# Moving the split weight tiles by 16 bytes, and the attention outputs by 128, within the scratch memory of a decoder trunk

## The chip, the cores and the metric

The kernel runs on one core of one Trainium2 chip. The metric is the device time in microseconds of one execution; the time before is the median of three runs, 2121.67 us (2117.71 to 2123.2).

## The reference

Two layers of a decoder trunk over 512 tokens of width 1024, one sequence. Each layer is a half-step SwiGLU FFN (hidden width 2816), a token mixer with three head groups in parallel (gated linear attention, native sparse attention, RetNet), and a second half-step FFN. Each sub-layer reads an RMS-normed, modulated input and adds a gated result; the modulation (nine vectors a layer) comes from a conditioning vector.

```
for l in range(2):
    mod = silu(c) @ w_ada[l] + b_ada[l]            # 9 x 1024
    x += 0.5 * gt1 * swiglu(modulate(rms_norm(x)), ffn1_in, ffn1_out)
    x += gtm * token_mixer(modulate(rms_norm(x)), w_in, ..., w_out)
    x += 0.5 * gt2 * swiglu(modulate(rms_norm(x)), ffn2_in, ffn2_out)
return rms_norm(x, final_norm_g)
```

All of it is float32.

## The kernel before, in words

Activations are kept transposed: `x` is 128 partitions by 8 chunks of the width by 512 tokens. The large products are done in TensorE's rounded float32 type (F32R) with a split: each operand is a rounded high part and a low part (the rest), and a product is three matmuls, high by high, high weight by low input, low weight by high input (`mm3`, lines 414 to 420). The inputs are split once into `hh`, `hl` (normed input), `gh`, `gl` (FFN hidden), `oh`, `ol` (linear attention outputs) and `nh`, `nl` (sparse attention outputs).

Weights come in units of 128 by 1024, some smaller. The class `Weights` streams them in the order of a list: `dma_to` loads a unit from DRAM into one of three `wraw` buffers on the SP queue; `split_to` rounds it on ScalarE into one of four `whi` buffers (line 170) and subtracts on VectorE, for a few units on GpSimd, into one of four `wlo` buffers (line 171). A unit is split two units ahead of its use, so there are normally 24 matmuls, eight slices of 128 weight columns by three, for each pair of split instructions. In an FFN, each unit's slices are the stationary operand and a 128x512 chunk of the input is the moving one. In the projections of `proj_n` (lines 578 to 580) and the small ones at 643 to 645 the roles are swapped: slices of the input are stationary, and `whi` and `wlo` move. Around the norms, FFN and output products run in halves of 256 tokens.

The order within an engine is that of the program, with a planner's priorities; tiles are laid out by pools in the 128 partitions' scratch memory, one after the other, in byte offsets common to all partitions. Constants come first from the left, then the `weights` pool (three wraw, four whi, four wlo, 4096 bytes a partition each), then `hh` and `hl`, then the pools of a stage. The FFN's pool (`gh`, `gl`), the mixer's `mix` pool and the `lin` pool (`oh`, `ol`, `nh`, `nl`) are laid out from the right end. In this layout the offsets modulo 256 are:

| tiles | offset modulo 256 |
|---|---|
| wraw, whi, wlo | 128 |
| hh, hl, gh, gl | 128 |
| qraw, qrot, krot, vnat, oh, ol, nh, nl | 0 |

The slices of a tile are 512 bytes (weights) or 1024 and 2048 bytes (inputs) apart, so all slices of a tile share its class; the exception is the units of lines 643 to 645, whose slices are 1696 bytes apart. `G` (the sparse attention's gates) uses 96 of the 120 elements it is given; it is the first tile of the `mix` pool from the right.

`load_consts` loads the constants; its later part (`late`) is built behind the first products: DMAs on GpSimd's queue, a cast of the causal mask to bf16, memsets. `onat` holds the natural-order outputs of the two linear attentions; `lin_evac` writes it first, at line 859.

Of the kernel before, what the change touches and what calls it, by code (L numbers as in the profile page):

```python
# [7 lines left out]
F32 = mybir.dt.float32  # L8
F32R = mybir.dt.float32r
# [9 lines left out]
L, D, T, F = 2, 1024, 512, 2816  # L19
# [120 lines left out]
class Weights:  # L140
# [21 lines left out]
    def split_to(self, i):  # L162
        while self.ns < len(self.units) and self.ns <= i:
            j = self.ns
            self.dma_to(j)
            _, w, pool = self.units[j]
            r = self.raw.pop(j)
            h = self.pool.tile([128, D], F32R, name="whi", tag="whi", bufs=self.b)
            lo = self.pool.tile([128, D], F32R, name="wlo", tag="wlo", bufs=self.b)
            self.nc.scalar.activation(h[:, :w], r[:, :w], AF.Copy)  # L170
            (self.nc.gpsimd if pool else self.nc.vector).tensor_tensor(lo[:, :w], r[:, :w], h[:, :w].bitcast(F32),  # L171
                                                                       op=ALU.subtract)
            self.hl[j] = (h[:, :w], lo[:, :w])
            self.ns += 1
# [11 lines left out]
class Build:  # L186
# [19 lines left out]
    def load_consts(self):  # L206
        nc, cp, a = self.nc, self.const, self.a
        self.ones = cp.tile([128, 128], F32, name="ones")
        nc.vector.memset(self.ones, 1.0)
        self.scratch = cp.tile([128, 1], F32, name="scratch")  # L210
        self.eps = cp.tile([128, 1], F32, name="eps")
        nc.vector.memset(self.eps, EPS)

        def ld0(key, shape, dt=F32, eng=None):
            t = cp.tile(shape, dt, name="k_" + key)
            (eng or nc.scalar).dma_start(t, a[key])
            return t

        self.ident = ld0("k_ident", [128, 128])
        self.bada = ld0("bada", [128, L, NADA * KC])  # L220
        self.ng = ld0("ng", [128, L, 3, KC])

        def late():
            def ld(key, shape, dt=F32):
                return ld0(key, shape, dt, nc.gpsimd)

            self.fng = ld("fng", [128, KC])
            self.kd = ld("k_kd", [128, 4])
            self.gc = ld("k_gc", [128, 2])
            self.cma = ld("k_cma", [128, 4, 32])  # L230
            self.cmm = ld("k_cmm", [128, 32])
            self.ab = ld("ab", [128, L, 2])
            causal = ld("k_causal", [128, 128])
            self.causal = cp.tile([128, 128], BF16, name="causal")
            nc.gpsimd.tensor_copy(self.causal, causal)
            self.identb = cp.tile([128, 128], BF16, name="identb")
            nc.gpsimd.tensor_copy(self.identb, self.ident)
            self.vb = cp.tile([128, 4, 128], F32, name="vb")
            nc.gpsimd.memset(self.vb, 0.0)
            self.hv = cp.tile([128, 2, 2, 32], F32, name="hv")  # L240
            nc.gpsimd.memset(self.hv, 0.0)
            self.onat = cp.tile([128, 4, 2, 256], F32, name="onat")
            self.sg = cp.tile([128, 4, 2, 256], F32, name="sg")
            self.stats = cp.tile([128, 2, 2, 4, 2], F32, name="stats")
            self.kcT = cp.tile([128, 2, 32], F32, name="kcT")
            nc.gpsimd.memset(self.kcT, 0.0)
        self.late_consts = late
# [346 lines left out]
    def mixer(self, l):  # L594
        nc, tc = self.nc, self.tc
        self.mp_cm = tc.tile_pool(name="mix", bufs=1, side="right", reuse_waits="tile")
        mp = self.mp = self.mp_cm.__enter__()
# [1 line left out]
        qrot = mp.tile([128, 4, T], F32, name="qrot")  # L599
        krot = mp.tile([128, 2, T], F32, name="krot")  # L600
        vnat = mp.tile([128, 4, 256], F32, name="vnat")
        G = mp.tile([128, 120], F32, name="G")[:, 0:96].rearrange("p (c k) -> p c k", c=4)
        onat, sg, stats = self.onat, self.sg, self.stats
        with tc.tile_pool(name="mtmp", bufs=1, reuse_waits="tile") as tp:
            self.tp = tp
# [54 lines left out]
            for c in range(4):  # L660
                nc.vector.tensor_tensor(G[:, c, :], gl[:, c, 0:24], gb, op=ALU.add)
            nc.scalar.activation(G, G, AF.Exp, scale=-1.0)
            nc.vector.tensor_scalar(G, G, 1.0, None, op0=ALU.add)
            nc.vector.reciprocal(G, G)
            self.dbg(f"G{l}", G)
            self.dbg(f"kcT{l}", self.kcT)
# [12 lines left out]
            for pr in range(2):  # L679
                e = tp.tile([128, T], F32, name="e", tag="e", bufs=1)  # L680
                q = tp.tile([128, T], F32, name="rq", tag="rq", bufs=2)
                k = tp.tile([128, T], F32, name="rk", tag="rk", bufs=2)
                p = self.proj_t(l, f"gq{pr}")
                nc.scalar.activation(q, p, AF.Copy, scale=0.125)
                p = self.proj_t(l, f"gk{pr}")
# [8 lines left out]
            for pr in range(2):  # L694
                q = tp.tile([128, T], F32, name="rq", tag="rq", bufs=2)
                k = tp.tile([128, T], F32, name="rk", tag="rk", bufs=2)
                for t, n, s in ((q, "rq", 1.0), (k, "rk", 0.125)):
                    p = self.proj_t(l, f"{n}{pr}")
# [3 lines left out]
            for i, n in enumerate(("ks", "kw")):  # L702
                p = self.proj_t(l, n)
                raw = tp.tile([128, T], F32, name="raw", tag="raw", bufs=2)
                self.rotary(p, krot[:, i, :], raw, 1.0)
            for i in range(4):
                p = self.proj_t(l, f"nq{i}")
# [6 lines left out]
        self.ol = op.tile([128, 4, T], F32R, name="ol")  # L714
        self.nsa(l, qraw, qrot, krot, vnat, G)

# [526 lines left out]
```

## Time and profile before

| what | value |
|---|---|
| median of the runs | 2121.67 us |
| the profiled execution's own time | 2122.84 us |
| its span, first to last instruction | 2121.1 us |
| TensorE matmul busy | 2093.0 us, 99% |
| weight loads busy | 1743.2 us, 82% |
| VectorE, ScalarE, GpSimd busy | 52%, 38%, 10% |
| HBM read over the span | 124 GB/s with the writes |

A matmul's row in the profile has a duration that overlaps with the next one's, since matmuls are pipelined; two matmuls' starts give the time that one takes in a stream. The starts are in the timeline, in steps of 0.01 us, so a step is taken over several rows.

### The profile page before, as it was taken

The numbers are of one execution on the slowest core, as the hardware profiler recorded it, in microseconds if no ns is written. First come the engines' busy times: TensorE is split into PE (matmuls) and PEld (weight loads), VectorE is DVE, ScalarE is ACT, GpSimd is POOL, SyncE is SP. The second block draws the span as 40 slices with busy tenths as digits, with TensorE's granted clock in tenths as the row PEclk, the third lists the DMA queues.
The fourth block names the chain that finished last, engine by engine and source line by source line (L and its number), as shares of the span: only waits on it lengthen the run. The fifth ranks groups of instructions, "written<-read, shape, count | busy, mean of one in ns | idle before, by whom it ended". The sixth has DMA issues, their size and how long they took to land.

```text
span 2121.1 us, 27803 instructions
## 1 busy us (share of the span) xinstructions
PE 2093.0 (99%) x10938; PEld 1743.2 (82%) x10938; DVE 1108.0 (52%) x1731; ACT 796.3 (38%) x1309; POOL 211.0 (10%) x196
## 2 busy tenths in 40 slices
PE   9999999999999999999999999999999999999998
PEld 7888888988965988888888888889788669888887
DVE  8894333637875799533353333335578754333332
ACT  4422323543665522222342222234527654222323
POOL 1000001312301200000110000012223020000002
PEclk9999999999999999999999999999999999999999
DMA  9894323423310699432333233235232112233322
GB/s 342 310 358 156 91 83 100 144 90 96 96 40 19 236 359 339 159 99 78 91 110 93 82 114 99 75 98 166 82 90 79 31 35 85 91 89 113 96 80 80
DMA packets 93829, 269.10 MB, mean 127 GB/s; under 512 B 10865, under 2 KB 21985, under 8 KB 93698
## 3 DMA queue, kind: packets, MB, share of 16 engines
q1 hardware_dynamic: 92018, 266.06, 38.7%
q8 instruction: 86, 1.41, 0.3%
q0 software_dynamic: 672, 0.58, 0.2%
q10 hardware_dynamic: 1008, 0.69, 0.1%
q14 instruction: 45, 0.37, 0.0%
HBM read 259.94 MB, written 2.10 MB: 124 GB/s over the span
## 4 chain that ended last, share of the span: by engine, by line
PE 96%; DVE 2%; ACT 1%; issue 1%; POOL 0%; DMA 0%; POOLq 0%; DVEq 0%; ACTq 0%
PE mm L418 26%; PE mm L419 26%; PE mm L420 26%; PE o L1062 2%; PE mm L579 1%; PE t L1052 1%; PE mm L578 1%; PE mm L580 1%; PE mm L1020 1%; PE f L419 1%; PE f L418 1%; PE f L420 1%; PE mm L1021 1%; DVE hl L349 0%; PE o L756 0%
## 5 line engine op out<-in xcount | busy, mean ns | idle before, releaser
L170 ACT ACTIVATE whi<-wraw 128x1024 fp32r<-128x1024 f32 (+3 forms) x374 | 361.1, 966 | 1054.8 <-PE mm L419 971.8
L419 PE MATMUL mm<-hl,whi 128*128 128x512 f32 (+1 forms) x1736 | 654.8, 378 | 3.1 <-DVE hl L349 3.1
L420 PE MATMUL mm<-hh,wlo 128*128 128x512 f32 (+1 forms) x1736 | 654.5, 378 | 0.0
L418 PE MATMUL mm<-hh,whi 128*128 128x512 f32 (+1 forms) x1736 | 649.3, 378 | 2.8 <-ACT hh L378 2.2
L171 DVE TENSOR_TENSOR wlo<-wraw,whi 128x1024 fp32r<-128x1024 f32 (+2 forms) x354 | 390.7, 1104 | 447.7 <-ACT whi L170 440.6
L419 PEld LDWEIGHTS mm<-hl,whi 128*128 128x128 f32 x1736 | 328.6, 189 | 62.4 <-DVE hl L349 3.7
L418 PEld LDWEIGHTS mm<-hh,whi 128*128 128x128 f32 x1736 | 326.5, 189 | 64.0 <-issue 3.1
L420 PEld LDWEIGHTS mm<-hh,wlo 128*128 128x128 f32 x1736 | 328.3, 189 | 60.5 <-issue 2.0
L419 PE MATMUL mm<-gl,whi 128*128 128x512 f32 (+1 forms) x792 | 290.2, 366 | 0.0
L420 PE MATMUL mm<-gh,wlo 128*128 128x512 f32 (+1 forms) x792 | 289.6, 366 | 0.0
L418 PE MATMUL mm<-gh,whi 128*128 128x512 f32 (+1 forms) x792 | 289.1, 365 | 0.0
L301 POOL TENSOR_TENSOR sqa<-sqa,sq 128x512 f32<-128x512 f32 (+1 forms) x44 | 51.3, 1165 | 1433.2 <-ACT sq L300 1125.8
L544 DVE TENSOR_TENSOR sg<-sg,mm 128x512 f32<-128x512 f32 x85 | 58.4, 687 | 227.5 <-PE mm L420 225.0
L256 DVE SCALAR_TENSOR_TENSOR adaw<-adaw,cact 128x1024 f32<-128x1024 f32 x144 | 171.7, 1217 | 6.6 <-ACT cact L1150 6.6
L419 PEld LDWEIGHTS mm<-gl,whi 128*128 128x128 f32 x792 | 149.4, 189 | 24.3
L420 PEld LDWEIGHTS mm<-gh,wlo 128*128 128x128 f32 x792 | 149.4, 189 | 24.0
L418 PEld LDWEIGHTS mm<-gh,whi 128*128 128x128 f32 x792 | 149.4, 189 | 24.0
L426 DVE SCALAR_TENSOR_TENSOR x<-mm,mod,x 128x512 f32<-128x512 f32 (+1 forms) x94 | 63.0, 671 | 136.5 <-PE mm L420 136.5
L1027 ACT ACTIVATE p<-mm,nm 128x128 f32<-128x128 f32 (+3 forms) x128 | 66.4, 532 | 18.9 <-DVE nm L1024 18.7
L579 PE MATMUL mm<-wlo,hh 128*128 128x256 f32 x256 | 72.9, 285 | 0.0
L578 PE MATMUL mm<-whi,hh 128*128 128x256 f32 x256 | 72.9, 285 | 0.0
L580 PE MATMUL mm<-whi,hl 128*128 128x256 f32 x256 | 72.7, 284 | 0.0
(289 smaller groups left out, 2145.2 us busy)
## 6 DMA issues: line engine op xcount, KB each, us to landing
wraw<-wfi SPq DMA_DIRECT2D x176, 512.0 KB, 3.7
adaw<-wada SPq DMA_DIRECT2D x144, 512.0 KB, 5.6
wraw<-wfo SPq DMA_DIRECT2D x64, 384.0 KB, 3.1
wraw<-wfo SPq DMA_DIRECT2D x64, 320.0 KB, 2.9
wraw<-wt SPq DMA_DIRECT2D x30, 512.0 KB, 3.7
wraw<-wn SPq DMA_DIRECT2D x16, 512.0 KB, 3.8
w<-w SPq DMA_DIRECT2D x16, 256.0 KB, 5.3
wraw<-wol SPq DMA_DIRECT2D x8, 512.0 KB, 3.7
```

The costliest lines, as they stand in the source:

```text
L170: self.nc.scalar.activation(h[:, :w], r[:, :w], AF.Copy)
L171: (self.nc.gpsimd if pool else self.nc.vector).tensor_tensor(lo[:, :w], r[:, :w], h[:, :w].bitcast(F32), op=ALU.subtract)
L256: i = nc.vector.scalar_tensor_tensor(w, w, 1.0, self.cact, op0=ALU.mult, op1=ALU.mult, accum_out=self.mod[l][:, f:f + 1])
L418: nc.tensor.matmul(out, wh[:, wk], hh[:, hk], start=start, stop=False)
L419: nc.tensor.matmul(out, wh[:, wk], hl[:, hk], start=False, stop=False)
L420: nc.tensor.matmul(out, wl[:, wk], hh[:, hk], start=False, stop=stop)
L426: nc.vector.scalar_tensor_tensor(xd, p, gate, xd, op0=ALU.mult, op1=ALU.add)
L544: nc.vector.tensor_tensor(sg, sg, pu, op=ALU.mult)
L578: nc.tensor.matmul(o, self.hh[:, k, ts], wh[:, cs], start=(k == 0 and c % 2 == 0), stop=False)
L579: nc.tensor.matmul(o, self.hh[:, k, ts], wl[:, cs], start=False, stop=False)
L580: nc.tensor.matmul(o, self.hl[:, k, ts], wh[:, cs], start=False, stop=(k == KC - 1 and c % 2 == 1))
L1027: nc.scalar.activation(p[:, h, :], s[:, i, :], AF.Exp, bias=nm[:, h:h + 1], accum_out=sm[:, h:h + 1])
```

## The change

The buffers of `whi` and `wlo` get 64 elements (256 bytes) more, and the data begins 4 elements (16 bytes) into them. `onat` is laid out earlier, and the causal mask is loaded into a part of it instead of a tile of its own, which frees 512 bytes. `G` is given 152 elements instead of 120 (608 bytes instead of 480). After it the offsets modulo 256 are 144 for the data of whi and wlo, and 128 for wraw, hh, hl, gh, gl, qraw, qrot, krot, vnat, oh, ol, nh and nl.

```diff
-            h = self.pool.tile([128, D], F32R, name="whi", tag="whi", bufs=self.b)
-            lo = self.pool.tile([128, D], F32R, name="wlo", tag="wlo", bufs=self.b)
+            h = self.pool.tile([128, D + 64], F32R, name="whi", tag="whi", bufs=self.b)[:, 4:4 + D]
+            lo = self.pool.tile([128, D + 64], F32R, name="wlo", tag="wlo", bufs=self.b)[:, 4:4 + D]
...
-            causal = ld("k_causal", [128, 128])
+            self.onat = cp.tile([128, 4, 2, 256], F32, name="onat")
+            causal = self.onat[:, 0, 0, 0:128]
+            nc.gpsimd.dma_start(causal, a["k_causal"])
...
-            self.onat = cp.tile([128, 4, 2, 256], F32, name="onat")
...
-        G = mp.tile([128, 120], F32, name="G")[:, 0:96].rearrange("p (c k) -> p c k", c=4)
+        G = mp.tile([128, 152], F32, name="G")[:, 0:96].rearrange("p (c k) -> p c k", c=4)
```

## Rows read from the trace of the kernel before

**Rows 1.** The page: busy us, share of the span, instructions; granted clock in 40 slices.
```profile
PE 2093.0 (99%) x10938; PEld 1743.2 (82%) x10938; DVE 1108.0 (52%) x1731; ACT 796.3 (38%) x1309; POOL 211.0 (10%) x196
...
PEclk9999999999999999999999999999999999999999
```

**Rows 2.** The page: chain that ended last, share of the span by engine.
```profile
PE 96%; DVE 2%; ACT 1%; issue 1%; POOL 0%; DMA 0%; POOLq 0%; DVEq 0%; ACTq 0%
```

**Rows 3.** Timeline (start us, us, instruction), TensorE, first layer's second FFN, 512 columns.
```profile
919.22 0.39 PE L420 MATMUL mm<-hh,wlo 128*128 128x512 f32 x1
...
921.26 0.39 PE L420 MATMUL mm<-hh,wlo 128*128 128x512 f32 x1
```

**Rows 4.** Timeline, TensorE, the next FFN's first products, 256 columns.
```profile
1075.82 0.28 PE L420 MATMUL mm<-hh,wlo 128*128 128x256 f32 x1
...
1077.26 0.28 PE L420 MATMUL mm<-hh,wlo 128*128 128x256 f32 x1
```

**Rows 5.** Timeline, weight loads, around a norm's one-column products (four loads a row).
```profile
694.28 0.53 PEld L314 LDWEIGHTS st<-ones,sqa 128*128 128x128 f32 x4
...
695.17 0.19 PEld L418 LDWEIGHTS mm<-nh,whi 128*128 128x128 f32 x1
```

**Rows 6.** Timeline of the first products; and a window (us, busy us by engine, PEclk, DMA, GB/s).
```profile
22.45 0.63 PE L419 MATMUL mm<-hl,whi 128*128 128x512 f32 x1
...
24.16 0.63 PE L419 MATMUL mm<-hl,whi 128*128 128x512 f32 x1
...
18.00:24.00 6.00, 5.13 (x12) 4.08 (x13) 5.13 (x11) 3.17 (x5) 0.00 (x0) 0.51 1.09 366
```

**Rows 7.** Timeline, TensorE, the sparse attention's output product, 512 columns.
```profile
676.92 0.39 PE L418 MATMUL mm<-nh,whi 128*128 128x512 f32 x1
...
679.48 0.40 PE L418 MATMUL mm<-nh,whi 128*128 128x512 f32 x1
```

**Rows 8.** Timeline, the same product in its halves, 256 columns.
```profile
687.03 0.29 PE L419 MATMUL mm<-nl,whi 128*128 128x256 f32 x1
...
688.58 0.28 PE L420 MATMUL mm<-nh,wlo 128*128 128x256 f32 x1
```

**Rows 9.** Groups of TensorE by form (busy us, mean ns); one row of each triple.
```profile
L420 PE MATMUL mm<-hh,wlo 128*128 128x512 f32 x1512 | 591.0, 391 | 0.0
...
L420 PE MATMUL mm<-gh,wlo 128*128 128x512 f32 x616 | 239.6, 389 | 0.0
...
L579 PE MATMUL mm<-wlo,hh 128*128 128x256 f32 x256 | 72.9, 285 | 0.0
...
L420 PE MATMUL mm<-hh,wlo 128*128 128x256 f32 x224 | 63.5, 288 | 0.0
...
L420 PE MATMUL mm<-gh,wlo 128*128 128x256 f32 x176 | 50.0, 284 | 0.0
...
L420 PE MATMUL f<-oh,wlo 128*128 128x512 f32 x64 | 25.4, 397 | 0.0
L420 PE MATMUL mm<-nh,wlo 128*128 128x512 f32 x40 | 15.8, 394 | 0.0
...
L644 PE MATMUL mm<-wlo,hh 128*128 128x296 f32 x48 | 14.0, 299 | 0.0
...
L420 PE MATMUL mm<-nh,wlo 128*128 128x256 f32 x48 | 13.5, 281 | 0.0
```

**Rows 10.** Timeline, TensorE, 512 columns just behind other products.
```profile
434.53 0.39 PE L419 MATMUL mm<-hl,whi 128*128 128x512 f32 x1
...
436.38 0.39 PE L418 MATMUL mm<-hh,whi 128*128 128x512 f32 x1
```

**Rows 11.** Groups of the page (busy us, mean ns, idle before and what ended it).
```profile
L171 DVE TENSOR_TENSOR wlo<-wraw,whi 128x1024 fp32r<-128x1024 f32 (+2 forms) x354 | 390.7, 1104 | 447.7 <-ACT whi L170 440.6
```

**Rows 12.** The tiles causal and onat (min/median/max ns, first and last start).
```profile
L235 POOL CAST causal<-k_k_causal x1: 387/387/387, 10.7 to 10.7; 128x128 bf16<-128x128 f32 x1
...
L859 ACT ACTIVATE onat<-t x4: 597/597/599, 471.4 to 1553.7; 128x512 f32<-128x512 f32 x4
```

## The prediction, made before the change was run

> **What bounds the kernel now.** Read the page's busy times first: TensorE is busy for 2093.0 us of a 2121.1 us span, and its clock is at full speed almost throughout [rows 1]. The chain of waits says the same from the other end: 96% of the time that ended last is TensorE's own work, with 2% for VectorE and 1% for ScalarE [rows 2]. So the time is the number of matmuls times the step from one matmul's start to the next. Their printed durations overlap and are no price; the steps are read from the timeline.
>
> In the middle of an FFN the starts of 128x512 matmuls run from 919.22 to 921.26 us in nine steps: 226.7 ns each [rows 3]. With 256 columns twelve steps take 1.44 us: 120.0 ns each [rows 4]. The difference, 106.7 ns for 256 columns, is 2.4 columns per ns, so 512 columns need 213.3 ns and 256 need 106.7. In both lengths the same 13.3 ns is left over at each hand-over. I call this the surplus. The weight load beside it is not the reason by its length: in front of one-column matmuls eight loads take 694.28 to 695.17 us, 111 ns each [rows 5], below both steps. And in the short stretch with a granted clock of 0.51, the 1.2 GHz level, four steps of 512 columns take 1.71 us, 427.5 ns, against 426.7 ns for the columns alone [rows 6]: there the surplus is 1 ns or less. So it belongs to reads at the full rate, not to the instruction.
>
> Does an address move it? One place says yes. The classes below are byte offsets modulo 256, as the tiles are laid out. For hh, hl, gh and gl as moving operand and whi, wlo as weights, both classes are 128. For oh, ol, nh and nl the moving class is 0 and the weights' is 128. With nh and nl the same 512-column triple takes 2.56 us for eleven steps, 232.7 ns: a surplus of 19.4 ns [rows 7]. With 256 columns it is 1.55 us over 13 steps, 119.2 ns: a surplus of 12.6 [rows 8]. The steps there are uneven, while those of rows 3 are even. The distance between the class of the weights and that of the moving operand therefore has a price on this chip, of 6 ns one way and 0.7 the other.
>
> **The change part by part.** *Weights behind the class.* Each whi and wlo buffer grows from 4096 to 4352 bytes, 17 times 256, and its data begins 16 bytes in. wraw, hh, hl, gh and gl stay at class 128; whi and wlo go to class 144. Every split-product matmul now has a distance of 16 where it had 0 (in the projections with swapped roles it is the moving side that is 16 ahead). No instruction is added or removed. The trace has distances of 0 and 128 in numbers, never 16, so the new surplus must be bounded. Below: 0, as in the half-speed stretch [rows 6]; for 256 columns no less than 4.3 ns, since the loads repeat every 111 ns [rows 5]. Above: 19.4 ns, the uneven steps of rows 7. I take half of today's, 6.7 ns for both lengths: rows 3 and 4 show that one surplus serves both, and 6.7 lies between the load's floor of 4.3 and the settled 13.3.
>
> The counts by shape [rows 9]: 3 x (1512 + 616) = 6384 matmuls of 512 columns and 3 x (256 + 224 + 176) = 1968 of 256, all with distance 0 today, and 3 x 48 = 144 of 296 columns (the few in the o, f and t banks are left out).
> - 512 columns: 6384 x 6.7 ns = 42.8 us.
> - 256 columns: 1968 x 6.7 ns = 13.2 us.
> - 296 columns: 144 x 6.7 ns = 1.0 us.
>
> *Attention outputs into the same class.* G grows from 480 to 608 bytes. It is the last of its pool's tiles toward the right end, so vnat, krot, qrot, qraw and the four outputs all move by 128 bytes, from class 0 to 128. Their 3 x (64 + 40) = 312 matmuls of 512 columns go from a surplus of 19.4 to 6.7: 4.0 us. Their 3 x 48 = 144 of 256 columns go from 12.6 to 6.7: 0.8 us [rows 7 to 9]. The other readers of these tiles (scores, transposes, the apply products) have two-pass or bf16 products whose steps are the load's or a releaser's; I take nothing, and bound it by 2 us either way, some 400 matmuls at 5 ns.
>
> *The causal mask loaded into onat.* The DMA has the same queue, rows and bytes, and POOL's cast the same shape. New is that the first writer of onat must find the cast done. The cast runs at 10.7 us, the first write of onat at 471.4 us [rows 12]: hidden by 460 us.
>
> *Everything moved.* The left pools grow by 2048 - 512 = 1536 bytes, so mixer tiles overlap other retired FFN tiles than before. The waits for them can differ at the four changes of stage. All of TensorE's idle time is 2121.1 - 2093.0 = 28 us [rows 1]; I take nothing and allow 4 us either way. ScalarE and VectorE write whi and wlo at the new offset. The split on VectorE takes 1104 ns [rows 11], one per 24 matmuls or 5.4 us; even doubled it would stay hidden.
>
> Sum: 42.8 + 13.2 + 1.0 + 4.0 + 0.8 = 61.8 us. TensorE is idle for 1.3% of the span, and where another engine ends the wait a faster stream only waits longer, so I take off 3%: 60 us. From the profiled execution, 2122.8 us (its span is 2121.1), that leaves 2062.9. It stood 1.2 us above the median of the runs, so the time on their scale is 2062 us. Next behind TensorE would be VectorE at 52% of the span: no new bound.
>
> One rule speaks against the whole change. The Trainium skill (TensorE: Matmul & The Clock Gate, "Step-by-step: what each phase is for") says that TensorE reads the moving operand and the weights through two independent ports, and that loading the next weights takes no read bandwidth from the running matmul. By that rule no distance matters and the time stays. Rows 3 and 7 differ by 6.0 ns in the same shapes with only the classes moved, so the trace does not bear the rule out fully; it keeps the chance of the second rival below.
>
> **The rivals.**
> 1. *The two reads no longer meet at all.* The surplus goes to its floor: 0 for 512 columns, 4.3 for 256. Gain: 6384 x 13.3 + 1968 x 9.0 + 144 x 13.3 + 312 x 19.4 + 144 x 8.3 = 84.9 + 17.7 + 1.9 + 6.1 + 1.2 = 112 us, so about 2010 us. For it: rows 6 show a hand-over without surplus. Against it: no full-speed step of this kernel is that short. The Trainium skill (same page, "Back-to-back issue gap") gives 2.5 ns over the columns at full clock; with that for 512 and 296 columns it would be 2027 us, as an estimate by that page.
> 2. *The surplus settles where it was.* 13.3 ns is the same for two lengths and returns after every disturbance: at 434.53 to 436.38 us, just behind other work, eight steps average 231 ns [rows 10], and later ones are back at 226.7. What always returns to one value may do so for a distance of 16 too. Then only the outputs change: 312 x 6.1 - 144 x 0.7 = 1.8 us, so 2120 us.
> 3. *The steps no longer settle* (the other side). Distance 0 is the even case, and rows 7 show what a distance without an even course costs. If 16 is such a distance, every 512-column step goes from 226.7 to about 232.7 and every 256-column one from 120.0 to 119.2: 6384 x 6.0 - 1968 x 0.8 = 36.7 us more, and the outputs keep theirs: 2159 us. It decides as soon as the mean 512-column step in the FFNs is above 226.7 ns. Against it: 16 bytes are a small move and 128 the largest.
>
> **How the numbers follow.** Forecast (surplus about halved, between 4.5 and 9 ns): 0.44, 2062 us, own range 2045 to 2085. Rival 1: 0.14. Rival 2: 0.16. Rival 3: 0.23. The last 0.03 is for placement that adds waits, on the slower side. A measurement of this kernel can tell about 0.3%, 6.4 us, from no change. Faster: 0.44 + 0.14 = 0.58; same: 0.16; slower: 0.23 + 0.03 = 0.26. The range 2030 to 2160 takes in the forecast, rival 2 and the better half of rival 3. It leaves out the strongest gains, some 0.08, and the worse half of rival 3, some 0.11.
>
> **What would show it.** The timeline of an FFN stretch with 512 columns: about 220 ns a step by the forecast, under 217 by rival 1, 226.7 by rival 2, 230 or more and uneven by rival 3. The 256-column stretches: 113 ns by the forecast. With nh and nl the step should be that of hh and hl in every case but rival 3; if it stays at 232.7 while the FFN's falls, the class of the outputs is not what set it. Counts, the granted clock and the work of ScalarE and VectorE should be unchanged. The prediction is wrong if the 512-column step moves by less than 1 ns or rises.

## The result, and the profile after

The changed kernel takes 2147.65 us (median of 4 runs, 2145.88 to 2158.19), the kernel before 2120.52 us (median of 4, 2117.71 to 2123.2). The ratio is 1.0135, with a 95% interval from 1.0103 to 1.0166: it is slower by 1.35%, where 2062 us, a gain of 2.8%, was forecast. The profile is that of the 2158.19 us run, the slowest of the four; a second profile of it (e5, below) shows where its extra 10 us lie. Against the profiled 2122.84 us of before it is 35.3 us longer.

The page of the changed kernel: busy us, share and count of each engine; the granted clock in 40 slices; the chain by engine; and the group of the split on VectorE.

```profile
PE 2128.8 (99%) x10938; PEld 1746.5 (81%) x10938; DVE 1108.1 (51%) x1731; ACT 796.4 (37%) x1309; POOL 211.2 (10%) x196
...
PEclk9999999999999999999999999999999999999999
...
PE 96%; DVE 2%; ACT 1%; issue 1%; POOL 0%; DMA 0%; POOLq 0%; DVEq 0%; ACTq 0%
...
L171 DVE TENSOR_TENSOR wlo<-wraw,whi 128x1024 fp32r<-128x1024 f32 (+2 forms) x354 | 390.7, 1104 | 466.8 <-ACT whi L170 459.6
```

Read it against [rows 1, 2, 11]: every count is the same, the clock is the same, the split takes the same 1104 ns, the chain has the same shares. TensorE's idle time is 2156.4 - 2128.8 = 27.6 us where it was 28. All of the 35 us is in TensorE's busy time, with the same number of matmuls: the steps are longer.

The timeline of the changed kernel (start us, us, instruction), 512 columns in an FFN, which answers to [rows 3]:

```profile
932.57 0.39 PE L419 MATMUL mm<-hh,whi 128*128 128x512 f32 x1
932.80 0.40 PE L420 MATMUL mm<-hl,whi 128*128 128x512 f32 x1
933.04 0.39 PE L421 MATMUL mm<-hh,wlo 128*128 128x512 f32 x1
933.27 0.39 PE L419 MATMUL mm<-hh,whi 128*128 128x512 f32 x1
933.50 0.40 PE L420 MATMUL mm<-hl,whi 128*128 128x512 f32 x1
933.74 0.40 PE L421 MATMUL mm<-hh,wlo 128*128 128x512 f32 x1
933.97 0.39 PE L419 MATMUL mm<-hh,whi 128*128 128x512 f32 x1
```

Six steps in 1.40 us are 233.3 ns, where they were 226.7: the surplus went from 13.3 to 20.0 ns. The steps are even, each 0.23 or 0.24 us in these rows; the price of the worst rival came without its unevenness. The 256-column products of the next FFN, over 25 steps, which answer to [rows 4]:

```profile
1092.40 0.28 PE L421 MATMUL mm<-hh,wlo 128*128 128x256 f32 x1
...
1095.36 0.28 PE L419 MATMUL mm<-hh,whi 128*128 128x256 f32 x1
```

2.96 us over 25 are 118.4 ns, a surplus of 11.7 where it was 13.3. And the output product with nh and nl, 12 steps, which answers to [rows 7]:

```profile
685.64 0.40 PE L420 MATMUL mm<-nl,whi 128*128 128x512 f32 x1
...
688.44 0.40 PE L421 MATMUL mm<-nh,wlo 128*128 128x512 f32 x1
```

2.80 us over 12 are 233.3 ns: the outputs got the FFN's step, but the FFN's step came up to theirs.

The account, from the starts of all steps that nothing else interrupts (mean surplus in ns, before and after, times their count):

```
512 columns, hh/hl   13.57 -> 19.68   x 4541   +27.7 us
512 columns, gh/gl   13.33 -> 20.00   x 1848   +12.3 us
256 columns, swapped 13.22 -> 10.57   x  730    -1.9 us
256 columns, hh/hl   13.2  -> 11.7    x  529    -0.8 us
256 columns, gh/gl   13.12 -> 11.65   x  500    -0.7 us
sum                                            +36.6 us   (measured: 35.3)
```

### The profile page after: what moved, and what is told of

It is laid out like the page before. It is cut to its first block, busy times and chain, and to the rows that moved or that the text cites. A ratio compares the mean times of both kernels' runs of the same rounds, so it can differ in the third digit from the quotient of the medians.

```text
span 2156.4 us, 27806 instructions
## 1 busy us (share of the span) xinstructions
PE 2128.8 (99%) x10938; PEld 1746.5 (81%) x10938; DVE 1108.1 (51%) x1731; ACT 796.4 (37%) x1309; POOL 211.2 (10%) x196
## 4 chain that ended last, share of the span: by engine, by line
PE 96%; DVE 2%; ACT 1%; issue 1%; POOL 0%; DMA 0%; POOLq 0%; DVEq 0%; ACTq 0%
PE mm L420 26%; PE mm L419 26%; PE mm L421 26%; PE o L1063 2%; PE t L1053 1%; PE mm L580 1%; PE mm L579 1%; PE mm L581 1%; PE mm L1021 1%; PE f L420 1%; PE f L419 1%; PE f L421 1%; PE mm L1022 1%; PE o L757 0%; DVE hl L350 0%
## 5 line engine op out<-in xcount | busy, mean ns | idle before, releaser
L420 PE MATMUL mm<-hl,whi 128*128 128x512 f32 (+1 forms) x1736 | 665.6, 384 | 3.0 <-DVE hl L350 3.0
L421 PE MATMUL mm<-hh,wlo 128*128 128x512 f32 (+1 forms) x1736 | 662.1, 382 | 0.0
L171 DVE TENSOR_TENSOR wlo<-wraw,whi 128x1024 fp32r<-128x1024 f32 (+2 forms) x354 | 390.7, 1104 | 466.8 <-ACT whi L170 459.6
L419 PEld LDWEIGHTS mm<-hh,whi 128*128 128x128 f32 x1736 | 330.9, 192 | 74.9 <-issue 3.1
L420 PE MATMUL mm<-gl,whi 128*128 128x512 f32 (+1 forms) x792 | 295.0, 372 | 0.0
L1028 ACT ACTIVATE p<-mm,nm 128x128 f32<-128x128 f32 (+3 forms) x128 | 66.5, 532 | 18.9 <-DVE nm L1025 18.7
```

Source lines behind the costliest of these rows:

```text
L419: nc.tensor.matmul(out, wh[:, wk], hh[:, hk], start=start, stop=False)
L420: nc.tensor.matmul(out, wh[:, wk], hl[:, hk], start=False, stop=False)
L421: nc.tensor.matmul(out, wl[:, wk], hh[:, hk], start=False, stop=stop)
L1028: nc.scalar.activation(p[:, h, :], s[:, i, :], AF.Exp, bias=nm[:, h:h + 1], accum_out=sm[:, h:h + 1])
```

## The experiments

**e1: the change without its 16 bytes.** Padding, mask in onat, larger G and moved pools stay.

```diff
-... name="whi", tag="whi", bufs=self.b)[:, 4:4 + D]
+... name="whi", tag="whi", bufs=self.b)[:, 0:0 + D]     (wlo likewise)
```

> The changed kernel with the data of whi and wlo at the start of their padded buffers: class 128 again, distance 0, while the larger buffers, the mask in onat, the larger G and every moved pool stay. Distance theory: the 16 bytes alone cost the time, so the 512-column step is 226.7 ns again, in the output products too (232.7 before), and the time is that of before less some 2 us: about 2118 us. Rival, placement: the loss lies in the moved pools, the mask or the waits that these bring; then the time stays near 2147 us.

Measured: 2120.82 us (10 runs, 2118.39 to 2122.82) against 2122.36 (13 runs); ratio 0.9995 [0.9985, 1.0004]. The FFN's 512-column surplus is back at 13.56 and 13.33. The whole loss hangs on the 16 bytes; all else together costs nothing that can be measured. The outputs alone, in class 128 with weights of class 128 (e1's timeline, 12 steps):

```profile
675.73 0.39 PE L420 MATMUL mm<-nl,whi 128*128 128x512 f32 x1
...
678.45 0.39 PE L421 MATMUL mm<-nh,wlo 128*128 128x512 f32 x1
```

2.72 us over 12 are 226.7 ns, where [rows 7] have 232.7 for the same product. So the class of the outputs is what set their step, as the prediction read it. The gain is about 1 us over the kernel (nh/nl 18.97 to 13.95, oh/ol 18.9 to 17.0), under what can be told.

**e2, e3: the surplus by distance, alone.** A small kernel with nothing but the split product in a stream, 48 matmuls a distance; the trunk isn't computed.

```
for k in range(8):
    for w, h in ((wh, hh), (wh, hl), (wl, hh)):      # all tiles in one class
        matmul(p[:, 0:n], w[:, dw + 128*k : dw + 128*k + 128], h[:, dm + 512*(k % 6) : ... + n])
```

> Not the trunk: only split-product matmuls in one stream, with nothing else on the chip's engines, with the output a copy of the input. Segments a: 512 columns, weights 0 to 240 bytes behind the inputs' class in steps of 16. Segments b: the same with 256 columns. Segments c: both shifted by the same 16, 48, 128 or 176 bytes. Segments e: some distances of a again in another order. Distance theory: the step follows the distance: 226.7 ns at 0 and in all of c, 231 to 234 at 16 and 232 at 128, with 256 columns 120 at 0 and 118 to 119 at 16; some distance may be below 226. Rival, another engine: ScalarE and VectorE writing or reading the shifted tiles slow TensorE's reads; then all segments of a show one step, and so do those of b.

> Only split-product matmuls in one stream, output a copy of the input. 512 columns: weights and inputs each 0 to 240 bytes behind their class in steps of 16, 256 pairs of 24 matmuls; then 256 columns, both in steps of 32, 64 pairs. Distance theory as first put (the difference of the two classes alone decides): every pair with the same difference has the same step, 226.7 ns for all with difference 0. Rival (the stream runs on a grid of about 6.67 ns in time, and the inputs' own class matters too): the steps settle at 226.7 or 233.3 ns with few values between, shifts of both by 32, 64 or 128 bytes keep the step and odd multiples of 16 do not; with 256 columns 113.3, 116.7 or 120 ns. Neither theory has a 512-column step under 226 ns; one at 220 would be a version to try.

Measured, surplus in ns by distance, that is by the number of bytes, modulo 256, that the weights lie behind the moving operand. The lines marked e2 are its first pass, in order; the line marked e3 is the mean of all pairs whose moving operand lies at a multiple of 32 bytes (without the very first pair, in which the kernel starts up):

```
distance    0   16   32   48   64   80   96  112  128  144  160  176  192  208  224  240
512, e2  13.3 13.3 20.0 20.0 20.0 18.5 21.1 20.0 20.0 20.0 20.0 16.7 15.5 20.0 20.0 13.3
512, e3  13.3 13.3 20.0 20.0 20.0 18.8 21.0 20.0 20.0 20.2 20.1 16.3 15.5 20.0 20.1 13.3
256, e2  13.3 11.7 11.7 11.1  6.7 12.0 12.1 13.1 12.2 13.3 13.3 11.5  6.7 10.0 10.0 13.3
```

Distance 32 in e2's timeline, six steps in 1.40 us, where distance 0 has 226.7 ns a step:

```profile
44.09 0.40 PE L45 MATMUL a<-hh,wh 128*128 128x512 f32 x1
...
45.49 0.40 PE L45 MATMUL a<-hh,wh 128*128 128x512 f32 x1
```

Three things follow. No distance of all 256 pairs gives 512 columns less than 13.3 ns: the forecast's 6.7 and the first rival's 0 exist nowhere, and distance 0 is already the best. For 256 columns 6.7 does exist, at 64 and 192, but it is not the price of these distances: in e3 two of the eight pairs at 64 have 6.7 and six have 11.1, and all eight at 192 have 11.2; in e4 the addresses of e2 give 11.2 and 11.1. Distance 64 with 256 columns, 12 steps each, first e2, then e4:

```profile
217.39 0.28 PE L45 MATMUL b<-hl,wh 128*128 128x256 f32 x1
...
218.75 0.28 PE L45 MATMUL b<-hl,wh 128*128 128x256 f32 x1
...
311.70 0.28 PE L46 MATMUL t<-hl,wh 128*128 128x256 f32 x1
...
313.12 0.28 PE L46 MATMUL t<-hl,wh 128*128 128x256 f32 x1
```

They are 1.36 us and 1.42 us, 113.3 and 118.3 ns. And at 16, the very distance of the change, the stream shows 13.3 where the kernel shows 20.0. That missed what was expected, and a theory with one value for each distance can't hold against it. e2 gave the hint: distance 144 read 20.0 in its first pass and 13.3 in a later one in another order, and 192 read 15.5 and then 20.0. A distance can have two values. (Where the moving operand lies at an odd multiple of 16, distance 0 itself gives 17.8 to 20.0, and 16 mostly still 13.3. So the distance alone isn't the whole rule, as e3's theory had it; nor do all of e2's segments shifted together have 226.7 ns: shifted by 16, 48 and 176 bytes they have surpluses of 20.0, 17.8 and 17.8.)

**e4: lengths.** The same stream with fewer weight columns, other column counts, and offsets inside 16 bytes.

> The same stream. Segments m: 512 columns, weight slices of 128, 96, 64 and 32 columns, at distances 0 and 128. If the surplus comes from the weight load's reads beside the matmul's, it falls with the weight columns, to some 3 ns or less at 32; if it is the matmul's own, it stays at 13.3. Segments n: distance 0, 512 down to 240 columns. With a grid of 6.67 ns the step stays a multiple of it, 226.7 for 512 to 500 and 220 for 496; with a fixed cost the step falls with every column, 225.0 for 508. Segments s and t: weights 4 to 28 bytes (and 64 to 72, 192) behind, 512 and 256 columns: within 16 bytes the step should be that of 0 (226.7, 120.0) if lines of 16 bytes are what is read, and differ if not.

Measured at distance 0, weights of 128, 96, 64, 32 columns: surplus 13.3, 16.7, 16.7, 18.3; at 128 bytes: 18.8, 13.3, 15.8, 17.7. The weight loads of e4 (busy us, mean ns) and 13 steps with 32 columns:

```profile
L46 PEld LDWEIGHTS m<-hh,wh 128*128 128x128 f32 x32 | 6.4, 205 | 13.8 <-ACT wh L24 12.3
...
L46 PEld LDWEIGHTS m<-hh,wh 128*32 128x32 f32 x32 | 3.5, 109 | 3.9
```

```profile
100.97 0.40 PE L46 MATMUL m<-hl,wh 128*32 128x512 f32 x1
...
103.97 0.40 PE L46 MATMUL m<-hh,wl 128*32 128x512 f32 x1
```

The load's printed time halves, the step becomes longer (3.00 us over 13 are 231 ns). So the surplus isn't time that a load's length takes: that theory of mine falls. By column count the step is 226.67 for 512 and for 504, 223.33 for 500, 220.00 for 488, 216.67 for 480, 173.33 for 384, 146.67 for 320, 120.00 for 256, 116.67 for 252, 112.0 for 240. At distance 0 the step is a whole number of 3.33 ns for 10 of the 14 lengths (not for 508, 448, 248 and 240); 504 columns cost what 512 do, and 508 some 228 ns, more than 512. So both forecasts for the lengths missed: a grid of 6.67 ns has no 223.33, and a fixed cost would have made 508 columns shorter, 225.0. Four and eight bytes of distance, inside 16, give 19.2 and 17.3 with 512 columns, and not the step of 0, as lines of 16 bytes would have had it.

**e5: the changed kernel, profiled again.**

> The changed kernel once more, for a second profile. Two-values theory: at a distance of 16 the 512-column step settles at 233.3 or at 226.7 ns, by what came before; the runs of 2146 us have more stretches at 226.7 than the profiled one of 2158, 12 us / 6.67 ns or some 1800 more of the 6700 such matmuls. Rival: the steps are the same as in the first profile and the 10 us lie in waits.

Measured: 2146.3 us. 140 us in each of the four FFNs (us, TensorE busy and matmuls, ..., PEclk, DMA share, GB/s); first the 2158 us run of the changed kernel, then this one:

```profile
100.00:240.00 140.00, 140.00 (x601) 113.37 (x600) 89.92 (x140) 35.20 (x45) 0.00 (x0) 1.00 0.66 230
880.00:1020.00 140.00, 140.00 (x602) 113.37 (x601) 46.77 (x52) 38.55 (x49) 0.00 (x0) 1.00 0.32 94
1200.00:1340.00 140.00, 140.00 (x601) 113.38 (x601) 46.52 (x52) 35.65 (x44) 0.00 (x0) 1.00 0.32 99
1880.00:2020.00 140.00, 140.00 (x601) 113.38 (x600) 45.84 (x52) 35.15 (x44) 0.00 (x0) 1.00 0.31 97
```

```profile
100.00:240.00 140.00, 140.00 (x601) 113.43 (x601) 89.75 (x140) 35.20 (x45) 0.00 (x0) 1.00 0.66 229
880.00:1020.00 140.00, 140.00 (x602) 113.43 (x601) 46.79 (x52) 38.51 (x48) 0.00 (x0) 1.00 0.31 95
1200.00:1340.00 140.00, 140.00 (x602) 113.44 (x601) 46.52 (x52) 35.62 (x44) 0.00 (x0) 1.00 0.32 98
1880.00:2020.00 140.00, 140.00 (x619) 116.00 (x618) 46.65 (x53) 36.19 (x45) 0.00 (x0) 1.00 0.34 101
```

619 matmuls in 140 us are 226 ns a step, 601 are 233. The last FFN of this run settled at the old step, with the same program. One FFN's unbroken stream has 1422 such matmuls: 1422 x 6.67 ns = 9.5 us of the 12 us between the two runs.

**e6: 64 bytes instead of 16.** `[:, 16:16 + D]` in both lines.

> The changed kernel with the data of whi and wlo 64 bytes into their buffers instead of 16. From the streams alone: 512 columns 233.3 ns (surplus 20.0 against 13.3: 6700 x 6.67 = 45 us more than before), 256 columns 113.3 ns (6.67 against 13.3: 2100 x 6.67 = 14 us less), so about 2150 us. If the distance is not what decides in the trunk, it stays within 6 us of before or of the changed kernel's 256-column steps of 116 to 120.

Measured: 2159.16 us (2 runs); ratio 1.0183 [1.0152, 1.0214]. All four FFNs have 601 or 602 matmuls in those windows: 20.0 ns, as the streams have it for 64. The 256-column surplus is 10.8, 9.0 and 11.1 (hh/hl, gh/gl, swapped) and not e2's 6.7, which e3 and e4 show to be the rarer value at 64. Of the 14 us expected there some 5 came.

**e7: one distance, many starts.** The stream again, 20 groups of 24 matmuls a distance, each behind one product of another length (132 to 246 columns), which shifts when the group begins.

> Only split-product matmuls of 512 columns in one stream, output a copy of the input. For each distance (0, 16, 240, 32, again 0 and 16, then 176 and 192 bytes) twenty groups of 24, each behind one product of another length (132 to 246 columns), which moves the point in time where the group starts. Two-values theory: at 0 every group comes back to 226.7 ns; at 16 some groups settle at 226.7 and some at 233.3 ns, by their start; at 240 likewise; at 32 all at 233.3. Rival: a distance has one step, and 16 shows 226.7 in all groups, as in the first stream; then something else in the trunk, not the distance, holds its matmuls at 233.3.

Measured: distance 0, all 20 groups at 226.7 ns; distance 32, all at 233.3; distance 240, 15 at 226.7 and 5 at 228.3; distance 16, 15 at 226.7 and 5 at 233.3, the same five groups in both of its passes; distance 176, all 20 at 230.0; distance 192, 19 at 228.9 and one at 233.3. Two neighbouring groups at distance 16, e7's timeline, 11 steps each: behind a product of 144 columns, and behind one of 150:

```profile
139.85 0.40 PE L46 MATMUL b<-hh,wh 128*128 128x512 f32 x1
...
142.42 0.40 PE L46 MATMUL b<-hh,wl 128*128 128x512 f32 x1
...
145.48 0.39 PE L46 MATMUL b<-hh,wh 128*128 128x512 f32 x1
...
147.98 0.39 PE L46 MATMUL b<-hh,wl 128*128 128x512 f32 x1
```

2.57 us and 2.50 us: 233.6 and 227.3 ns by the printed starts. Operands, addresses and instructions are the same; only what came before differs. Distance 16 has two settled steps, and distance 0 has one.

**e8: each product at the distance that suits it.** No offset for weights used with 512 columns, 64 bytes for those used with 256 only (in an FFN where `half == 0 and i < 2`, among others), 16 for the swapped ones (in `proj_n`).

```diff
-    def add(self, ap, width, pool=False):
+    def add(self, ap, width, pool=False, off=0):
...
-            ... name="whi", ...)[:, 4:4 + D]
+            ... name="whi", ...)[:, off:off + D]
...
+HALVES, SWAPPED = 16, 4
```

> The changed kernel with an offset by unit: 0 for the units used with 512 columns, 64 bytes for those used with 256 columns alone (the FFNs' first and last ones, the last of the attention output), 16 bytes for the projections with swapped roles. Distance theory: the 512-column steps stay at 226.7 ns, the 256-column ones fall from 120.0 to about 116 to 118, as in the changed kernels: 1970 x 2 to 4 ns, 4 to 8 us, so about 2114 us and 0.2 to 0.4% under before. Rival: units at different offsets next to each other disturb the settling, and the 512-column stretches behind them stay above 226.7; then it is not below before.

Measured: 2113.79 us (7 runs, 2113.05 to 2118.64) against 2122.16 (17 runs); ratio 0.9966 [0.9954, 0.9977]. This beats both kernels. The 512-column steps are as before; 51 steps of 256 columns ahead of an FFN:

```profile
1070.12 0.28 PE L420 MATMUL mm<-hh,whi 128*128 128x256 f32 x1
...
1076.13 0.28 PE L420 MATMUL mm<-hh,whi 128*128 128x256 f32 x1
```

6.01 us over 51 are 117.8 ns, against 120.0 in [rows 4]. Summed as in the account above, the 256-column steps return 4.7 us and the outputs 0.9, of the 8.4 us between the medians. The profiled execution is the slowest of the seven, 4.2 us below that of before; where the rest of the medians' difference lies is not shown.

**e9: 240 bytes, that is 16 the other way.** `[:, 60:60 + D]`.

> The changed kernel with the data 240 bytes into the padded buffers, 16 before the inputs' class. In the streams 240 had 226.7 ns with 512 columns and 118 to 120 with 256. Two-values theory: the trunk's disturbances send some stretches to 233.3, so between 2112 us (all at 226.7) and 2155 (all at 233.3), and not the same in each run. Rival, one value per distance: 226.7 throughout and 2112 to 2118 us, in every run.

Measured: 2119.35 us (8 runs); ratio 0.9989 [0.9979, 0.9999]. The 512-column surplus is 13.96 and 13.75 (some stretches at 226.7, some at 228.3 ns); the 256-column one is 10.5 to 11.6. The second value at this distance is only 1.7 ns above the first, as in e7, not 6.7, so I had expected too much loss. 16 bytes behind and 16 bytes ahead are not the same.

**e10, e11, e12: does the entry into an FFN pick the value?** Distance 16 stays for 512 columns; the 256-column products with weights of their own, which lead into each FFN, go to 0 (e10) or 64 (e11). e12 is the changed kernel in more runs, beside them.

```diff
-... name="whi", ...)[:, 4:4 + D]
+... name="whi", ...)[:, off:off + D]     (off = 4; 0 or 16 for the units used with 256 columns alone)
```

> The changed kernel with distance 16 kept for all products of 512 columns, and distance 0 for the 256-column products that lead into an FFN (and for the other 256-column products with weights of their own; the swapped ones stay at 16). Theory (a 512-column stream at distance 16 keeps the value that the entry gives it): another entry shifts the starts, so that the four FFN streams divide otherwise between 226.7 and 233.3 ns than three of four or four of four at 233.3; each stream that changes sides is 9.5 us, so the time is 2158 less a multiple of 9.5 us: 2139, 2130 or 2120 if two to four are low. Rival (the trunk's streams go to 233.3 whatever leads into them, through something within the FFN): three or four of four at 233.3 again, 2147 to 2159 us.

> As the run before, with 64 bytes in place of 0 for the 256-column products that lead into an FFN. Theory: the count of FFN streams at 226.7 ns differs from that of the changed kernel or of the run before; time 2158 less a multiple of 9.5 us, less some 1 us for the 256-column products. Rival: three or four of four at 233.3, 2146 to 2158 us.

> The changed kernel once more, as the measure for the two runs before. Theory: a profile with three or four FFN streams at 233.3 ns, and a median of 2146 to 2158 us, the runs falling into groups some 9.5 us apart. Rival (the difference between its runs isn't the streams' value): a spread without such groups.

Measured: e10 2157.28 us (2149.91 to 2158.84), e11 2154.77 (2153.88 to 2155.84), e12 2154.91 (2155.04, 2157.53, 2154.78, 2139.69). All four FFNs are at 233.3 ns in all three profiles; e11's:

```profile
100.00:240.00 140.00, 140.00 (x602) 113.37 (x601) 90.54 (x140) 35.20 (x44) 0.00 (x0) 1.00 0.67 231
880.00:1020.00 140.00, 140.00 (x602) 113.38 (x601) 46.81 (x52) 38.86 (x49) 0.00 (x0) 1.00 0.31 95
1200.00:1340.00 140.00, 140.00 (x601) 113.37 (x600) 46.56 (x52) 35.65 (x44) 0.00 (x0) 1.00 0.33 98
1880.00:2020.00 140.00, 140.00 (x602) 113.38 (x601) 45.84 (x52) 35.15 (x44) 0.00 (x0) 1.00 0.33 97
```

My theory that the products just ahead pick the value of a trunk's stream is not borne out in this form: with those products at other distances the streams still go to 233.3, as the rival said. The ten executions of the changed kernel in all (the four of the result, a fifth beside them at 2146.1 us, e5 and the four of e12) fall into groups: four from 2154.8 to 2158.2 us, five from 2145.9 to 2147.7, one at 2139.7. With 9.5 us for each FFN these fit none, one and two FFNs at 226.7. For the first two groups profiles show it; for 2139.7 there is none.

The traces of distance 16 show when a stream takes its value. In the five profiles (the first, e5, e10, e11, e12) every long stream, of 1422 to 1506 matmuls, keeps one step from its first two dozen matmuls to its last: 19 of the 20 are at 233.3 ns, and the last of e5 is at 226.7. Two short streams of the mixers, at the same distance and behind other products, have the same step each time: one of 66 matmuls at 481 us is at 226.7 in all five, one of 62 at 1547 us at 233.3 in all five. The first of them in the changed kernel, its second matmul and its last, 65 steps in 14.73 us, 226.6 ns:

```profile
481.41 0.39 PE L420 MATMUL mm<-hl,whi 128*128 128x512 f32 x1
...
496.14 0.39 PE L419 MATMUL mm<-hh,whi 128*128 128x512 f32 x1
```

So the value is fixed as a stream begins and is then held. The work of other engines beside it does not by itself raise the step: in e5's window at 1880 us VectorE and ScalarE work as much as in the others.

## Why the prediction was wrong

**The step that failed** is "I take half of today's, 6.7 ns for both lengths". Measured at distance 16: 20.0 ns (sometimes 13.3) for 512 columns, 11.7 for 256. Those two terms were to bring 42.8 and 13.2 us; the first costs some 40 us (27.7 + 12.3), the others return some 3.4. The value was an interpolation between a floor of another operation and today's surplus. It assumed that the surplus grows smoothly from a cause that an address can relieve. The tables of e2 and e3 show neither for 512 columns: most distances have one of two values, and distance 0 already has the lower one, the lowest that any pair has. The premise "that one surplus serves both" lengths fell with it, since 64 bytes give 20.0 for one, and 6.7 or 11.1 for the other.

**Rival 3** (0.23) had the right price, 36.7 us against the account's 36.6, and its sign to decide by, a mean step above 226.7 ns, decided. Its mechanism was only partly right. It said that the steps no longer settle and are uneven; they settle, evenly, at 233.3 ns. That is why the price fits so well: the uneven mean of [rows 7], 232.7, lies next to the second settled value; so far the price was luck. Its 2159 us is the kernel with all four FFNs there; the median of the first runs has, by its time and by e5's profile, one FFN at 226.7. What spoke against it in the prediction, "16 bytes are a small move and 128 the largest", was worth nothing: 32, 64 and 128 all give 20.0.

**Rival 2** has a part of the truth that I did not foresee: a stream at distance 16 can settle where it was (e7, the last FFN of e5). "Returns to one value" was read from distance 0, where every start does return, and does not hold at 16.

**Right** were: the bound (all of the difference is in TensorE's steps), that the classes of address set the step, that the outputs' class explains [rows 7] (e1), that mask, onat, G, moved pools and VectorE's split cost nothing, and that counts, clock and waits stay.

The rule of the Trainium skill (TensorE: Matmul & The Clock Gate, "Step-by-step: what each phase is for") of two independent ports is borne out in one respect and not in another: a load half as long takes nothing off the step (e4), but the addresses of the two operands do move it (e3). The Trainium skill (same page, "Back-to-back issue gap") gives 2.5 ns over the columns at full clock, for the gap of one matmul without the weight load beside it. The traces do not show it for these pairs of load and product: no settled 512-column step of these streams has less than 13.3, and the shortest 256-column one has 6.7.

**Open.** What the distance does inside the chip, why many settled steps are whole numbers of 3.33 ns, and what in its beginning sends a long stream of the trunk at distance 16 to 233.3 in 19 of 20 cases when the bare stream goes there in 5 of 20 starts. Not the cause are a price that falls with the length of the weight load (e4) and, for the trunk's streams, the class of the 256-column products just ahead (e10, e11). The exact time at which a stream begins, behind those products, was varied on purpose in the bare stream alone (e7).

## What to carry to other kernels

Where TensorE is the bound, read its step from starts in the timeline, and test an address by a stream of a few microseconds for each distance before laying out a kernel by it: the value between two measured ones need not lie between them. A small stream can still show only one of two settled values, so start it many times, and prefer a layout at which every start gives the same step. Lay weights out by the length of the product that uses them, as e8 does (0.34%), not by one offset for all.

## What the runs showed of the hardware

- Many settled steps of split fp32r products are multiples of 3.33 ns: 226.67, 233.33, 120.00, 113.33; at distance 0 it is so for 10 of 14 lengths, and 504 columns take as long as 512 (e4).
- 512 columns, moving operand at a multiple of 32 bytes: 13.3 ns over the columns at equal classes, 20.0 at most distances; nothing below 13.3 in all 256 pairs (e3). 256 columns: 13.3 at equal classes; at 64 bytes 6.7 in e2 and in two of e3's eight pairs, 11.1 in the others and in e4.
- One program, the same addresses: a stream of 1422 matmuls ran at 233.3 ns in one execution and at 226.7 in another (e5), 9.5 us in all. A stream that has begun at one of the two steps keeps it to its end (five profiles).
- A weight load of 32 columns in place of 128 makes the step longer, 231 ns for 226.7 (e4).
